# Front of a hybrid attention block: second-half transposes placed earlier, feature tiles copied and split in pairs; states of the linear heads split on DVE

## The chip, the cores and the metric

The kernel runs on one core of a Trainium2 chip. The engines are TensorE (PE, with its weight loads PEld), VectorE (DVE), ScalarE (ACT), GpSimd (POOL) and the queue that issues most loads (SP). Each engine works through its own instructions in order and waits on semaphores for the others. The metric is the device time of one execution in microseconds (us).

## What is computed

One block over 1024 tokens of width 1024, in fp32: a norm, one wide projection, three branches (retention, gated linear attention, windowed attention with sinks), gates, an output projection, and a feed-forward part.

```python
h = rmsnorm(x, norm_mix_pre)
proj = h @ w_in          # split into rq rk rv rg | gq gk gv gg ga | sq sk sv | gate_logits
o_ret = head_groupnorm(retention(rq, rk, rv)) * silu(rg)
o_gla = head_rmsnorm(gla(gq, gk, gv, log_a(ga))) * silu(gg)
o_swa = swa_sinks(sq, sk, sv, attn_sinks)
merged = sum(sigmoid(gate_logits) * einsum(branches, w_branch))
x = x + rmsnorm(merged @ w_out, norm_mix_post)
h = rmsnorm(x, norm_ffn_pre)
x = x + rmsnorm((silu(h @ ffn_w_gate) * (h @ ffn_w_up)) @ ffn_w_down, norm_ffn_post)
```

Retention and the gated branch go chunk by chunk: `state = decay * state + k^T v`, and each chunk's output adds `q` times the state before it.

## The kernel before, in words

Every fp32 operand of a matrix product is split into a high part (a cast on ACT, `fp32r`) and a low part (source minus high part, a subtraction on DVE); a product then takes three matmuls (high-high, high-low, low-high). The helper `split` does this at lines 127 and 128 of the profile.

**The front.** The 1024 tokens are two halves of 512 (`th` 0 and 1). For a half, four token tiles `x` are squared on ACT (`first_square`, which also sums), POOL makes `rstd`, DVE scales (`first_scale`, tile `xn`). PE then transposes to eight feature tiles (`k` 0 to 7): four 128x128 transposes fill one PSUM bank `xps`. `first_split` copies a bank to SBUF with the norm's gain (tile `hf`, odd `k` on DVE, even `k` on ACT) and splits it (tile `hT`: cast on ACT, subtraction on DVE). The products of the wide projection use a scheme with seven block products per pair of weight tiles ("key"); its steps are `p1` to `p7` with PSUM tiles `x`, `y`, `z`. They need splits of weight sums (`sums`: tiles `raw` and `s`) and of sums of the feature tiles of both halves (`t1` to `t4`; `make("t2")` makes `t2` first). `swa_values(t0)` makes the attention values of two token tiles: 48 matmuls of 272 columns into two banks `sv`, called four times (0, 2, 4, 6; the last two use the second half); ACT and DVE then split the result into `vhl`. In this front all engines keep the order in which the code is written (`e.on = True`), so its lines appear in the profile as L76. The order before is: first half, `p1` and `p2` of key 0 (the two `next(steps)`), split of the value weights on ACT and POOL, `swa_values(0)`, split of key 1's weights (`blocks`), `p1` and `p2` of key 1, `sums` of key 0, `swa_values(2)`, then the second half's eight transposed tiles with `sums` of key 1 in the middle, `t2`, `swa_values(4)`, `swa_values(6)`. After it, a scheduler orders the instructions.

**The linear heads.** Eight heads (four of retention, then four gated) run one after the other in `lin_head`, each over eight chunks. Per chunk DVE makes the new state `tmp` (tile `tu`, line 1041 or 1039) from the product `kv` and the state before; ACT makes its high part `us` (line 1045), DVE the low part (line 1046), POOL the scaled state `u` for the next chunk (line 1050). PE multiplies `us` with the queries of the next chunk (product `o<-us,q`). Between chunks `fill(1)` gives PE other products (values, or branch projections).

Of the kernel before, what the change touches and what calls it, by code (L numbers as in the profile page):

```python
# [11 lines left out]
AF = mybir.ActivationFunctionType  # L12
ALU = mybir.AluOpType
# [3 lines left out]
P = 128  # L17
# [3 lines left out]
NK = D // P  # L21
# [25 lines left out]
V_PRE, V_RW, V_RB, V_GW, V_FFN, V_BA, V_SNK, V_R, V_CAUSAL = 0, 8, 16, 24, 32, 40, 44, 60, 68  # L47
# [32 lines left out]
def block_kernel(ctx: ExitStack, tc: tile.TileContext, x, vecs, rows, alpha2, w_in, w_branch,  # L80
                 w_out, w_gate, w_up, w_down, cst_in, out):
    nc = tc.nc
    pe, ve, se, po = (Ordered(tc, e) for e in (nc.tensor, nc.vector, nc.scalar, nc.gpsimd))
# [15 lines left out]
    def bt(n, dt=F32):  # L99
        return bp.tile([P, TH], dt, name=f"{n}_{nid()}", tag="b")  # L100
# [7 lines left out]
    def bpair(n):  # L108
        t = dt_(n, F32R)
        return t[:, :TH], t[:, TH:]  # L110
# [3 lines left out]
    def bank(n):  # L114
        return psp.tile([P, TH], F32, name=f"{n}_{nid()}", tag="ps")
# [10 lines left out]
    def split(hi, lo, src, eng=None):  # L126
        se.copy(out=hi, in_=src)  # L127
        return (eng or ve).tensor_tensor(out=lo, in0=src, in1=hi, op=ALU.subtract)  # L128


    ident = const.tile([P, P], F32, name="ident")
    vec = const.tile([P, NVEC], F32, name="vec")
# [45 lines left out]
    def split_sv(raws):  # L178
        res = []
        for raw, kn in raws:  # L180
            wh, wl = wt_pair()
            split(wh[:, :kn * NSV], wl[:, :kn * NSV], raw[:, :kn * NSV], po)
            res += [(wh[:, k * NSV:(k + 1) * NSV], wl[:, k * NSV:(k + 1) * NSV]) for k in range(kn)]
        return res
# [102 lines left out]
    xT = [[None, None] for _ in range(NK)]  # L287
    hf = [[None, None] for _ in range(NK)]
# [9 lines left out]
    def first_square(xt):  # L298
        xn = dt_("xn")
        ms = sm("ms", 1)  # L300
        se.activation(out=xn, in_=xt, func=AF.Square, scale=1.0 / 32.0, accum_out=ms)
        return xn, rstd_of(ms, 1, EPS)
# [2 lines left out]
        ve.tensor_scalar(out=xn, in0=xt, scalar1=r, scalar2=None, op0=ALU.mult)  # L305
        return xn

    def first_split(k, th, ps):
        h = hf[k][th] = bt("hf")
        g = vec[:, V_PRE + k:V_PRE + k + 1]  # L310
        if k % 2:
            ve.tensor_scalar(out=h, in0=ps, scalar1=g, scalar2=None, op0=ALU.mult)
        else:
            se.activation(out=h, in_=ps, func=AF.Copy, scale=g)
        xT[k][th] = bpair("hT")
        split(*xT[k][th], h)


    ga = const.tile([P, NT, RANK], F32, name="ga")
# [2 lines left out]
    def swa_values(t0):  # L322
        ts = (t0, t0 + 1)
        pss = [bank("sv") for _ in ts]
        for k in range(NK):
            for t, ps in zip(ts, pss):
                hi, lo = (z[:, (t % 4) * P:(t % 4 + 1) * P] for z in xT[k][t // 4])
                mm3(ps[:, :NSV], (hi, lo), wsv[k], k == 0, k == NK - 1)
        v2 = dt_("vhl", F32R)
        for i, (t, ps) in enumerate(zip(ts, pss)):  # L330
            v = v2[:, i * TH:(i + 1) * TH].rearrange("p (g c) -> p g c", g=HKV)
            split(v[:, :, :DH], v[:, :, DH:], ps[:, :HKV * DH].rearrange("p (g c) -> p g c", g=HKV))
            ve.tensor_copy(out=ga[:, t, :], in_=ps[:, HKV * DH:NSV])
        po.dma_start(out=vhd[t0 // 2], in_=v2.bitcast(F32))
# [382 lines left out]
    inp = Pairs(mv, ikeys, in_load, in_out, 2, hsums)  # L717
# [11 lines left out]
    xns = []  # L729
# [5 lines left out]
        for k in range(NK):  # L735
            pe.transpose(out=pss[k][:, j * P:(j + 1) * P], in_=xns[j][:, k * P:(k + 1) * P], identity=ident)
    sq = []
    for k in range(NK):
        first_split(k, 0, pss[k])
        if k % 4 == 3:  # L740
            sq += [first_square(xt) for xt in xs2[k // 2 - 1:k // 2 + 1]]
    xns = [first_scale(xt, *q) for xt, q in zip(xs2, sq)]
    next(steps)
    next(steps)
    wsv = split_sv(wsv)
    swa_values(0)
    inp.blocks(ikeys[1])
    next(steps)
    next(steps)
    inp.sums(ikeys[0])  # L750
    swa_values(2)
    for k in range(NK):
        ps = bank("xps")
        for j in range(4):
            pe.transpose(out=ps[:, j * P:(j + 1) * P], in_=xns[j][:, k * P:(k + 1) * P], identity=ident)
        first_split(k, 1, ps)
        if k == 3:
            inp.sums(ikeys[1])
    inp.make("t2")
    swa_values(4)  # L760
    swa_values(6)
# [251 lines left out]
    def lin_head(br, h, st, fill):  # L1013
        if br == 0:
            to_end = lambda c: rret[:, h:h + 1]
            to_mid = lambda c: rret[:, H + h:H + h + 1]
        else:
            to_end = lambda c: gates_gla[h][0][:, c:c + 1]
            to_mid = lambda c: gates_gla[h][1][:, c + 1:c + 2]
        qs, ns, as_ = st["s"]  # L1020
        vs = st["v"]
        part = lambda pair, c: tuple(z[:, (c % 4) * P:(c % 4 + 1) * P] for z in pair[c // 4])
        u = uhl = None
        ys = [dt_("y"), dt_("y")]
        for c0 in range(0, NT, 2):
            pkv = bank("kv")
            po_ = bank("o")
            for c in (c0, c0 + 1):
                e = slice((c - c0) * DV, (c - c0 + 1) * DV)
                if c < NT - 1:  # L1030
                    mm3(pkv[:, e], part(ns, c), vs[c], True, True)
                mm3(po_[:, e], part(as_, c), vs[c], True, c == 0)
                if c:
                    mm3(po_[:, e], part(qs, c), uhl, False, True)
                if c < NT - 1:
                    tu = bt("tu")
                    tmp, un = tu[:, :DV], tu[:, DV:]
                    if u is None:
                        ve.tensor_scalar(out=tmp, in0=pkv[:, e], scalar1=to_end(c), scalar2=None, op0=ALU.mult)
                    else:  # L1040
                        ve.scalar_tensor_tensor(out=tmp, in0=pkv[:, e], scalar=to_end(c), in1=u,
                                                op0=ALU.mult, op1=ALU.add)
                    us = br_("us")
                    uhl = us[:, :DV], us[:, DV:]
                    se.activation(out=uhl[0], in_=tmp, func=AF.Copy, scale=to_mid(c))
                    ve.scalar_tensor_tensor(out=uhl[1], in0=tmp, scalar=to_mid(c), in1=uhl[0], op0=ALU.mult,
                                            op1=ALU.subtract)
                    if c < NT - 2:
                        u = un
                        po.tensor_scalar(out=u, in0=tmp, scalar1=to_mid(c), scalar2=to_end(c + 1),  # L1050
                                         op0=ALU.mult, op1=ALU.mult)
                if c == NT - 1:
                    se.copy(out=ys[1][:, 2 * DV:], in_=po_)
                fill(1)
            if c0 < NT - 2:
                se.copy(out=ys[c0 // 4][:, (c0 % 4) * DV:(c0 % 4 + 2) * DV], in_=po_)
            if c0 == 2:
                lin_norm(br, ys[0])
        lin_norm(br, ys[1])
        return [lambda th=th: lin_out(br, h, th, ys[th]) for th in range(2)]  # L1060
# [347 lines left out]
```

## Time and profile before

| | |
|---|---|
| median of 3 runs (lowest to highest) | 2171.03 us (2167.98 to 2172.43) |
| profiled execution: its time, its span | 2171.05 us, 2169.3 us |
| mean granted PE clock | 0.988 |
| PE busy | 2097.6 us (97%) |
| DVE, ACT, POOL busy | 1232.4 us (57%), 924.0 us (43%), 273.5 us (13%) |

The span runs from the first instruction to the last of the profiled execution. Busy time counts work alone, without waits. The granted clock is a share of TensorE's 2.4 GHz; 0.5 is its lower level, 1.2 GHz.

### The profile page before, as it was taken

The page shows a single profiled execution, that of the slowest core. Times are in us where ns is not written, and L with a number is a line of the kernel's source. Part 1 is how long each engine was busy: PE and PEld are TensorE (multiplying, and loading weights), DVE is VectorE, ACT ScalarE, POOL GpSimd, SP SyncE. Part 2 cuts the span into 40 slices and gives each one's busy share as a digit, 9 for nine tenths or more (in the row PEclk, how much of TensorE's full clock was granted, in tenths as well). Part 3 has the DMA queues.
Part 4 walks back from the last instruction along what each step waited for, and adds up shares of the span by engine and source line. Part 5 has one row for each costly group of instructions (what it writes and reads, how often), then busy time and mean ns, then how long its engine had stood idle before and what let it go on. Part 6 is the DMA issues. An engine that isn't in the chain of part 4 may idle for free. (4 is left out here: it accounts for less than half of the span.)

```text
span 2169.3 us, 28889 instructions
## 1 busy us (share of the span) xinstructions
PE 2097.6 (97%) x10612; PEld 1775.8 (82%) x10612; DVE 1232.4 (57%) x2263; ACT 924.0 (43%) x1800; POOL 273.5 (13%) x471
## 2 busy tenths in 40 slices
PE   6799999999999999999999999998999999999998
PEld 4678888888888899999788788876888888888886
DVE  4768764565443598755655744426765555553342
ACT  4446554334443577644533331145433333352240
POOL 2111000000000232232222210042000000000101
PEclk8999999999999999999999999999999999999999
DMA  4378665575556644576766654342454555574441
GB/s 150 116 225 262 195 193 161 183 228 180 171 156 191 215 149 149 176 244 238 271 226 234 221 178 134 107 126 88 134 154 132 139 146 141 149 278 142 154 171 39
DMA packets 351214, 376.64 MB, mean 174 GB/s; under 512 B 16848, under 2 KB 276304, under 8 KB 351072
## 3 DMA queue, kind: packets, MB, share of 16 engines
q1 hardware_dynamic: 309248, 273.59, 42.0%
q0 software_dynamic: 18208, 62.40, 7.6%
q10 hardware_dynamic: 23616, 38.81, 4.9%
q8 instruction: 83, 1.36, 0.3%
q14 instruction: 59, 0.48, 0.1%
HBM read 273.03 MB, written 101.71 MB: 173 GB/s over the span
## 5 line engine op out<-in xcount | busy, mean ns | idle before, releaser
L128 DVE TENSOR_TENSOR wl<-raw,wh 128x1024 fp32r<-128x1024 f32 x127 | 155.1, 1222 | 146.8 <-ACT wh L127 82.5
L127 ACT CAST s<-raw 128x512 fp32r<-128x512 f32 x216 | 130.1, 620 | 197.3 <-DVE raw L380 79.5
L127 ACT CAST wh<-raw 128x1024 fp32r<-128x1024 f32 x137 | 143.3, 1047 | 98.9 <-DMA raw<-in_w_down 52.0
L405 PE MATMUL x<-t,s 128*128 128x512 f32 x440 | 171.4, 392 | 5.6 <-ACT t L127 3.7
L406 PE MATMUL x<-t,s 128*128 128x512 f32 x440 | 172.8, 393 | 0.3 <-DVE t L128 0.3
L407 PE MATMUL x<-t,s 128*128 128x512 f32 x440 | 172.8, 393 | 0.4 <-DVE s L128 0.4
L355 ACT COPY sn<-x 128x512 f32<-128x512 f32 x163 | 95.2, 587 | 140.7 <-PE x L407 111.6
L241 PE MATMUL pf<-o,wh 128*128 128x512 f32 x384 | 149.8, 395 | 2.0 <-ACT o L127 2.0
L242 PE MATMUL pf<-o,wh 128*128 128x512 f32 x384 | 150.3, 392 | 0.4 <-DVE o L128 0.4
L128 DVE TENSOR_TENSOR s<-raw,s 128x512 fp32r<-128x512 f32 x216 | 145.4, 687 | 5.4 <-ACT s L127 4.6
L256 PE MATMUL v<-wh,hT 128*128 128x256 f32 x512 | 146.2, 285 | 0.0
L258 PE MATMUL v<-wh,hT 128*128 128x256 f32 x512 | 145.1, 283 | 0.0
L257 PE MATMUL v<-wl,hT 128*128 128x256 f32 x512 | 145.0, 283 | 0.0
L1340 PE MATMUL dn<-wl,f 128*128 128x512 f32 x352 | 136.3, 389 | 0.0
L1339 PE MATMUL dn<-wh,f 128*128 128x512 f32 x352 | 136.3, 389 | 0.0
L244 PE MATMUL pf<-o,wl 128*128 128x512 f32 x384 | 121.9, 391 | 0.0
L1342 PE MATMUL dn<-wh,f 128*128 128x512 f32 x352 | 108.7, 389 | 0.0
L405 PEld LDWEIGHTS x<-t,s 128*128 128x128 f32 x440 | 83.0, 189 | 24.0 <-ACT t L127 4.2
L257 PEld LDWEIGHTS v<-wl,hT 128*128 128x128 f32 x512 | 98.5, 192 | 1.1
L256 PEld LDWEIGHTS v<-wh,hT 128*128 128x128 f32 x512 | 98.4, 192 | 1.0
L258 PEld LDWEIGHTS v<-wh,hT 128*128 128x128 f32 x512 | 98.3, 192 | 0.1
L407 PEld LDWEIGHTS x<-t,s 128*128 128x128 f32 x440 | 83.5, 190 | 18.2 <-DVE s L128 0.8
(306 smaller groups left out, 5281.8 us busy)
## 6 DMA issues: line engine op xcount, KB each, us to landing
raw<-in_w_in SPq DMA_DIRECT2D x146, 512.0 KB, 6.0
raw<-in_w_down SPq DMA_DIRECT2D x44, 512.0 KB, 6.5
raw<-in_w_gate SPq DMA_DIRECT2D x43, 512.0 KB, 5.0
raw<-in_w_up SPq DMA_DIRECT2D x43, 512.0 KB, 4.6
v<-v POOLq DMA_DIRECT2D x32, 512.0 KB, 3.9
v<-v SPq DMA_DIRECT2D x32, 512.0 KB, 6.5
gT<-go ACTq DMA_DIRECT2D x48, 256.0 KB, 3.7
raw<-in_w_branch SPq DMA_DIRECT2D x24, 512.0 KB, 5.6
```

The source lines that it names most:

```text
L127: se.copy(out=hi, in_=src)
L128: return (eng or ve).tensor_tensor(out=lo, in0=src, in1=hi, op=ALU.subtract)
L241: pe.matmul(p_, lhsT=wh, rhs=hi, start=(k == 0), stop=False)
L242: pe.matmul(p_, lhsT=wh, rhs=lo, start=False, stop=False)
L256: pe.matmul(ps, lhsT=lh, rhs=rh, start=start, stop=False)
L257: pe.matmul(ps, lhsT=lh, rhs=rl, start=False, stop=False)
L258: pe.matmul(ps, lhsT=ll, rhs=rh, start=False, stop=stop)
L405: pe.matmul(ps, lhsT=h, rhs=hi, start=(start and k == 0), stop=False, skip_group_check=True)
L406: pe.matmul(ps, lhsT=h, rhs=lo, start=False, stop=False, skip_group_check=True)
L407: pe.matmul(ps, lhsT=l, rhs=hi, start=False, stop=(k == KH - 1), skip_group_check=True)
L1339: pe.matmul(ps[ch], lhsT=fh[:, ts_], rhs=ws[ch][0], start=(first and i == 0), stop=False)
L1340: pe.matmul(ps[ch], lhsT=fh[:, ts_], rhs=ws[ch][1], start=False, stop=False)
```

## The change

It does two things. In the front, `first_split` takes two banks: both are copied first (one on ACT, one on DVE), then both are split; a square of the second half follows every pair of the first half, in place of two squares behind every four tiles. The transposes of the second half are placed earlier: tiles 0 to 3 in front of `swa_values(0)`, tiles 4 to 7 in front of `p1` of key 1; `sums` of key 1 follows `swa_values(2)`. In `lin_head`, the high part of the state is made by DVE in place of ACT: 56 instructions of 128x256 (7 chunks of 8 heads).

```diff
-    def first_split(k, th, ps):
-        h = hf[k][th] = bt("hf")
-        g = vec[:, V_PRE + k:V_PRE + k + 1]
-        if k % 2:
-            ve.tensor_scalar(out=h, in0=ps, scalar1=g, scalar2=None, op0=ALU.mult)
-        else:
-            se.activation(out=h, in_=ps, func=AF.Copy, scale=g)
-        xT[k][th] = bpair("hT")
-        split(*xT[k][th], h)
+    def first_split(k0, th, pss):
+
+        for k, ps in zip((k0, k0 + 1), pss):
+            hf[k][th] = bt("hf")
+            g = vec[:, V_PRE + k:V_PRE + k + 1]
+            if k % 2:
+                ve.tensor_scalar(out=hf[k][th], in0=ps, scalar1=g, scalar2=None, op0=ALU.mult)
+            else:
+                se.activation(out=hf[k][th], in_=ps, func=AF.Copy, scale=g)
+        for k in (k0, k0 + 1):
+            xT[k][th] = bpair("hT")
+            split(*xT[k][th], hf[k][th])
...
-    for k in range(NK):
-        first_split(k, 0, pss[k])
-        if k % 4 == 3:
-            sq += [first_square(xt) for xt in xs2[k // 2 - 1:k // 2 + 1]]
+    for k in range(0, NK, 2):
+        first_split(k, 0, pss[k:k + 2])
+        sq.append(first_square(xs2[k // 2]))
...
+    def second_half(kk):
+        for k0 in kk:
+            pss = [bank("xps"), bank("xps")]
+            for k, ps in zip((k0, k0 + 1), pss):
+                for j in range(4):
+                    pe.transpose(out=ps[:, j * P:(j + 1) * P], in_=xns[j][:, k * P:(k + 1) * P], identity=ident)
+            first_split(k0, 1, pss)
+
     wsv = split_sv(wsv)
+    second_half((0, 2))
     swa_values(0)
     inp.blocks(ikeys[1])
+    second_half((4, 6))
     next(steps)
     next(steps)
     inp.sums(ikeys[0])
     swa_values(2)
-    for k in range(NK):
-        ps = bank("xps")
-        for j in range(4):
-            pe.transpose(out=ps[:, j * P:(j + 1) * P], in_=xns[j][:, k * P:(k + 1) * P], identity=ident)
-        first_split(k, 1, ps)
-        if k == 3:
-            inp.sums(ikeys[1])
+    inp.sums(ikeys[1])
     inp.make("t2")
...
-                    se.activation(out=uhl[0], in_=tmp, func=AF.Copy, scale=to_mid(c))
+                    ve.tensor_scalar(out=uhl[0], in0=tmp, scalar1=to_mid(c), scalar2=None, op0=ALU.mult)
```

Three places show how the rows on an engine move. First ACT in the first half, from its first copy out of PSUM; before:

```order
L76 ACTIVATE hf_291<-xps_251,vec 128x512
L76 CAST hT_293<-hf_291 128x512
L76 CAST hT_298<-hf_296 128x512
L76 ACTIVATE hf_301<-xps_253,vec 128x512
L76 CAST hT_303<-hf_301 128x512
L76 CAST hT_308<-hf_306 128x512
L76 ACTIVATE xn_311,ms_312<-x_198 128x1024
L76 ACTIVATE xn_317,ms_318<-x_200 128x1024
```

and in the changed kernel:

```order
L76 ACTIVATE hf_291<-xps_251,vec 128x512
L76 CAST hT_295<-hf_291 128x512
L76 CAST hT_298<-hf_293 128x512
L76 ACTIVATE xn_301,ms_302<-x_198 128x1024
L76 ACTIVATE hf_307<-xps_253,vec 128x512
L76 CAST hT_311<-hf_307 128x512
L76 CAST hT_314<-hf_309 128x512
L76 ACTIVATE xn_317,ms_318<-x_200 128x1024
```

ACT's own order within a pair stays; one square `xn` now follows each pair. On DVE (not shown) the odd tile's copy now stands ahead of the even tile's subtraction, where it stood behind it.

Second, ACT behind the second call of `swa_values`, whose result it casts to `vhl`; before, twelve rows of what follows:

```order
L76 CAST vhl_549<-sv_499 128x4x64
L76 CAST vhl_549<-sv_500 128x4x64
L76 ACTIVATE hf_562<-xps_557,vec 128x512
L76 CAST hT_564<-hf_562 128x512
L76 CAST hT_574<-hf_572 128x512
L76 ACTIVATE hf_582<-xps_577,vec 128x512
L76 CAST hT_584<-hf_582 128x512
L76 CAST hT_594<-hf_592 128x512
L76 CAST s_100_598<-raw_215 128x512
L76 CAST s_101_602<-raw_215 128x512
L76 ACTIVATE hf_612<-xps_607,vec 128x512
L76 CAST hT_614<-hf_612 128x512
```

and in the changed kernel:

```order
L76 CAST vhl_629<-sv_579 128x4x64
L76 CAST vhl_629<-sv_580 128x4x64
L76 CAST s_112_638<-raw_215 128x512
L76 CAST s_113_642<-raw_215 128x512
L76 CAST t_115_650<-t_114_647 128x512
L76 CAST t_117_656<-t_116_653 128x512
```

The copies `hf` and casts `hT` of the second half no longer stand between the values and `t2` (`t_115`); on DVE and PE it is the same.

Third, DVE in the last gated head, at the state of a chunk (`tu_12252`); before:

```order
L1041 SCALAR_TENSOR_TENSOR tu_12252<-kv_12241,end_2123,tu_12191 128x256
L128 TENSOR_TENSOR wl_12261<-raw_12258,wh_12260 128x1024
L1041 SCALAR_TENSOR_TENSOR tu_12287<-kv_12241,end_2123,tu_12252 128x256
L1046 SCALAR_TENSOR_TENSOR us_12254<-tu_12252,mid_2122,us_12254 128x256
L1046 SCALAR_TENSOR_TENSOR us_12289<-tu_12287,mid_2122,us_12289 128x256
```

and in the changed kernel:

```order
L1047 SCALAR_TENSOR_TENSOR tu_12252<-kv_12241,end_2123,tu_12191 128x256
L1051 TENSOR_SCALAR us_12254<-tu_12252,mid_2122 128x256
L128 TENSOR_TENSOR wl_12261<-raw_12258,wh_12260 128x1024
L1052 SCALAR_TENSOR_TENSOR us_12254<-tu_12252,mid_2122,us_12254 128x256
L1047 SCALAR_TENSOR_TENSOR tu_12287<-kv_12241,end_2123,tu_12252 128x256
L1051 TENSOR_SCALAR us_12289<-tu_12287,mid_2122 128x256
L1052 SCALAR_TENSOR_TENSOR us_12289<-tu_12287,mid_2122,us_12289 128x256
```

The high part (L1051) stands right behind the state, and the low part ahead of the next state. Before, the high part stood on ACT, where four scalings of `y` (line 992) were ahead of it at this place.

## Rows read from the trace of the kernel before

**Rows 1.** Page, part 1: busy time of each engine.

```profile
PE 2097.6 (97%) x10612; PEld 1775.8 (82%) x10612; DVE 1232.4 (57%) x2263; ACT 924.0 (43%) x1800; POOL 273.5 (13%) x471
```

**Rows 2.** Busy us of PE, PEld, DVE, ACT, POOL by stretch; clock, DMA share, GB/s.

```profile
35.00:43.30 8.30, 8.28 (x47) 8.06 (x47) 0.44 (x1) 0.36 (x1) 3.53 (x2) 0.71 0.01 2
43.30:58.80 15.50, 13.59 (x73) 11.78 (x74) 6.03 (x11) 3.33 (x7) 0.75 (x1) 0.89 0.08 34
58.80:78.00 19.20, 10.06 (x58) 8.63 (x57) 12.97 (x23) 9.11 (x16) 4.88 (x9) 0.73 0.37 138
78.00:95.70 17.70, 15.82 (x102) 13.84 (x100) 17.42 (x34) 8.19 (x17) 1.63 (x3) 1.00 0.37 116
95.70:140.00 44.30, 44.30 (x198) 36.13 (x199) 30.78 (x49) 21.57 (x38) 6.07 (x12) 1.00 0.74 227
905.00:1260.00 355.00, 345.13 (x2259) 308.89 (x2259) 212.81 (x443) 154.44 (x285) 97.88 (x173) 1.00 0.69 237
```

**Rows 3.** PE's longest wait from 40 us on, in the waits up to 96 us.

```profile
PE sv L76 <- ACT hf L76: 4.7, 1, 4.7
```

**Rows 4.** Timeline, first half: first copy, last low part, last square.

```profile
13.75 0.69 ACT L76 ACTIVATE hf<-xps,vec 128x512 f32<-128x512 f32 x1 [0.36 <-PE xps L76]
...
29.06 0.69 DVE L76 TENSOR_TENSOR hT<-hf,hT 128x512 fp32r<-128x512 f32 x1 [0.68 <-ACT hT L76]
...
29.98 1.04 ACT L76 ACTIVATE xn<-x 128x1024 f32<-128x1024 f32 x1
```

**Rows 5.** Groups by form, 0 to 96 us: high parts, scalings (count | busy, mean ns | idle before).

```profile
L76 ACT CAST hT<-hf 128x512 fp32r<-128x512 f32 x16 | 9.9, 618 | 12.2 <-DVE hf L76 11.9
...
L76 DVE TENSOR_SCALAR xn<-x,rstd 128x1024 f32<-128x1024 f32 x8 | 7.6, 956 | 11.5 <-POOL rstd L76 11.5
```

**Rows 6.** Timeline at 33 to 35 us: POOL's split, the last scaling, PE's start.

```profile
32.97 5.56 POOL L76 TENSOR_TENSOR wl<-raw,wh 128x816 fp32r<-128x816 f32 x3
33.05 2.39 DVE L76 TENSOR_SCALAR xn<-x,rstd 128x1024 f32<-128x1024 f32 x1 [0.77 <-POOL rstd L76]
34.95 0.59 PE L76 MATMUL sv<-wl,hT 128*128 128x272 f32 x1 [2.14 <-POOL wl L76]
```

**Rows 7.** Timeline of PE: third projection group, second transposes, the late z product.

```profile
52.69 0.28 PE L76 MATMUL sv<-wh,hT 128*128 128x272 f32 x1
...
58.70 2.47 PE L76 MATMUL xps<-ident,xn 128*128 128x128 f32 x20
...
95.69 0.50 PE L407 MATMUL z<-t,s 128*128 128x512 f32 x1 [1.00 <-DVE s L128]
```

**Rows 8.** Timeline of DVE: sums of key 1 begin, t2 begins, t2's last part.

```profile
66.65 0.68 DVE L76 TENSOR_TENSOR raw<-raw,raw 128x512 f32<-128x512 f32 x1
...
71.93 0.69 DVE L76 TENSOR_TENSOR hT<-hf,hT 128x512 fp32r<-128x512 f32 x1
...
77.85 0.69 DVE L76 TENSOR_TENSOR t<-hf,hf 128x512 f32<-128x512 f32 x1
...
90.29 0.68 DVE L76 TENSOR_TENSOR t<-t,t 128x512 fp32r<-128x512 f32 x1
```

**Rows 9.** PE's longest wait from 905 to 1260 us.

```profile
PE o L256 <- ACT us L1045: 4.8, 5, 1.8
```

**Rows 10.** Durations (min/median/max ns): ACT's split, POOL's u, a DVE scaling.

```profile
L1045 ACT ACTIVATE us<-tu,vec x28: 493/510/523, 916.4 to 1067.1; 128x256 fp32r<-128x256 f32 x28
...
L1050 POOL TENSOR_SCALAR tu<-tu,vec x24: 547/560/2297, 916.5 to 1056.7; 128x256 f32<-128x256 f32 x24
...
L866 DVE TENSOR_SCALAR lg<-lg,rs x128: 275/347/551, 726.3 to 901.2; 128x256 f32<-128x256 f32 x112, 128x128 f32<-128x128 f32 x16
```

**Rows 11.** Timeline, last head: the state, ACT's scalings of y, the late split.

```profile
1244.51 0.45 DVE L1041 SCALAR_TENSOR_TENSOR tu<-kv,end,tu 128x256 f32<-128x256 f32 x1
...
1247.64 1.70 ACT L992 ACTIVATE y<-y,rstd 128x256 f32<-128x256 f32 x4 [5.43 <-POOL rstd L141]
...
1249.25 0.89 ACT L1045 ACTIVATE us<-tu,mid 128x256 fp32r<-128x256 f32 x2
```

## The prediction

> **What bounds the kernel now.** I read the page first: PE is busy for 2097.6 us, 97% of the span [rows 1], so a change can only pay in the few places where PE waits or runs at its lower clock. The busy time by stretch shows one such place at the front [rows 2]: from 58.8 to 78 us PE is busy for 10.06 of 19.2 us at a mean granted clock of 0.73, a mixture of its two levels, 1.2 and 2.4 GHz. The list of PE's waits names what it waits for there: the values of the third token pair (`sv`) for the copies `hf` of the second half, 4.7 us in one piece [rows 3]. In the next stretch, up to 95.7 us, PE still waits now and then, and DVE is busy for 17.42 of 17.7 us: it makes `t2` and the splits behind it, so DVE's place in its queue sets when PE can go on. From 95.7 to 140 us PE has no gap at all (44.30 of 44.30 us) at full clock [rows 2]. So whatever brings the product at 95.69 us [rows 7] forward is carried on to the end. The second place is the stretch of the linear heads, where PE is busy for 345.13 of 355 us [rows 2] and its longest wait is for `us` from ACT, 4.8 us in five pieces [rows 9].
>
> **Part 1, the front.** I follow the chain in the new order, with durations of the old rows.
>
> First half. Before, copies and splits of the eight tiles run from 13.75 to 29.75 us and the last square ends at 31.02 [rows 4]. ACT's casts spend 11.9 us waiting for copies that DVE makes one subtraction late [rows 5]. With both copies ahead of the splits ACT has no such gap, and it is the longer queue: per pair a copy (0.69), two casts (0.62 each) and a square (1.04), 2.97 us. Four pairs from 13.75 end at 25.6: 5.4 us earlier.
>
> Last scaling. It started at 33.05, while POOL had begun to split the value weights at 32.97, and took 2.39 us [rows 6]; the other seven take (7.6 - 2.39)/7 = 0.74 us each [rows 5]. Shifted by 5.4 it starts at 27.65, again beside POOL. I take 2.39 again, the nearest row, so it ends at 30.0; the other bound, 0.74, would give 1.65 us more.
>
> Tiles 0 to 3 of the second half. Two pairs without squares: 2 x (0.69 + 0.62 + 0.62) = 3.9 us on ACT, done at about 34.9 with the last low part. PE needs only the transposes, some 2.6 us of them behind the last scaling, and starts the values (0) at 32.6 where it had started at 34.95 [rows 6]. Those 48 matmuls took up to 43.3 us at clock 0.71 [rows 2]; the group from 52.69 to 58.70 took 6.0 at full clock [rows 7]. With PE at work since 30.0 I take 7, so they end at 39.6 (bounds 6 and 8.3).
>
> Key 1 and values (2). Before, PE waited for the split of key 1's weights behind 43.3, did 24 products and was through at 52.69: 9.4 us. Now 16 transposes lie in that wait (20 take 2.47 us [rows 7], so 2.0); the products at full clock cost 24 x 44.3/198 = 5.4 [rows 2], and I leave 0.7 of the wait. The values follow with 6.0: 39.6 + 2.0 + 0.7 + 5.4 + 6.0 = 53.7, where it was 58.7. Tiles 4 to 7 are copied and split beside these products, on ACT and DVE, which were busy for only 3.33 and 6.03 us in 43.3 to 58.8 [rows 2]; without that cover they would put 2 x 1.93 = 3.9 us ahead of `t2`.
>
> `t2`. Behind the values (2) DVE had the second half's tiles with the sums of key 1 in their middle, and began `t2` only at 77.85 [rows 8]. Now only the sums are left (5.3 us, 66.65 to 71.93) and the values' own split (estimate 1.2, four short operations). `t2` itself takes 13.1, from 77.85 to 90.97 [rows 8]. So it ends at 53.7 + 1.2 + 5.3 + 13.1 = 73.3, which is 17.7 us earlier. What stands behind it is in the same order, so the product that waits for `s` at 95.69 comes at 78.0.
>
> What is given back. PE now finishes the values (6) at 53.7 + 12 = 65.7 and waits between the parts of `t2`, so I expect one spell at 1.2 GHz more behind it. The stretch at clock 0.89, with waits of PE at its start, lost at most 15.5 x 0.11 = 1.7 us by the lower level; the one at 0.73 lost at most 19.2 x 0.27 = 5.2, half of it in gaps [rows 2]. I take 2.2. Part 1: -17.7 + 2.2 = -15.5 us. Its best end has the short scaling, the values (0) at 6 and no spell: -20.3. Its worst is that only PE's gaps from 58.8 to 78 go: 19.2 - 10.06 = -9.1. The writes of `hT` by POOL also start earlier, ahead of the values' writes; their data are there by 34.9, so they hold nothing.
>
> **Part 2, the heads.** Removed: 56 operations of 0.51 us on ACT; added: 56 on DVE. This trace has no such operation in the heads; the nearest row is a DVE scaling of the same shape, 0.35 us at the median [rows 10], so DVE gets 19.6 us more in 355, where it is busy for 212.81 [rows 2]. Behind the new instruction on DVE wait the low part, the next state and splits for other products. The gain: ACT takes its instructions in order, and at the end of the last head the state is there at 1244.96, but four scalings of `y`, which wait for POOL's `rstd`, come first at 1247.64, and `us` starts only at 1249.25 [rows 11]. On DVE it would start at 1245. At most the 4.8 us of this wait go; at the other end all 19.6 us lie on PE's path. Since PE has other products between chunks, I take -3.5, and for the range -4.8 to +3.
>
> POOL's `u` starts from the same state as the moved operation, and takes 0.56 us [rows 10]. The last scaling of the front shows what an overlap with POOL costs DVE: 2.39 in place of 0.74 us. The Trainium skill (Advanced Engine Details and Errata, "VectorE Performance Modes", Mode Summary) says that DVE's second port is shared with GpSimd, that DVE's two-port modes and GpSimd's instructions block each other, and that such a mode wants source and result in SBUF, as they are here. By that rule this part is no gain but the loss that stands below as a rival; the trace agrees with it in that one row. The scalings of the same shape at 0.275 to 0.551 us [rows 10] show no such hold in their length, so I leave it at a small chance.
>
> **Sum.** The profiled execution took 2171.05 us (span 2169.3 and 1.75 around it), next to the median of 2171.03. 2171.05 - 15.5 - 3.5 = 2152 us.
>
> **The rivals.**
> (a) As forecast: 2152, with a range of its own from 2146 to 2158. Chance 0.70.
> (b) The front gives less: the spells at the lower clock come at the key's products too, or DVE reaches `t2` later, so that little more than PE's gaps goes, and the heads give nothing: 2171 - 9.1 = 2162. For it: the clock fell behind a short wait at the same weights before (0.89). Against it: 16 transposes now stand there. Chance 0.17.
> (c) The change doesn't do what it says, because the gain is given back before 140 us: DVE, busy for 30.78 of 44.3 us there, or the loads of the next weights set the pace. For it: DMA is at 0.74 in that stretch. Against: PE has no gap there, and loads start when buffers come free, which also comes earlier. Between 2168 and 2171. Chance 0.08.
> (d) Slower, by one mechanism: the moved operation is held by POOL's `u` for its 0.56 us and then needs 0.35, so 0.91 us of DVE's queue per chunk. If PE pays all of it, 56 x 0.91 = 51 us; half of it, 25, gives 2171 - 15.5 + 25 = 2181. It decides from 0.35 us per chunk on, since 56 x 0.35 = 19.8 is what outweighs part 1 and 0.2%. Against: PE's own work between chunks. Chance 0.05.
>
> **How the numbers follow.** 0.2% of 2171 is 4.3 us, about what a measurement of this kernel can tell from no change. Cases (a) and (b) are faster, 0.87; (c) is the same, 0.08; (d) is slower, 0.05. The range takes in the best ends of both parts (2171 - 20.3 - 4.8 = 2146) and (b) with a loss of 3 in the heads (2171 - 9.1 + 3 = 2165); (c) and (d) lie outside.
>
> **What would show it.** In the changed profile the last square of the second half should end near 25.6 us, the values (0) near 39.6, `t2` near 73, and the product that waits for `s` should start near 78 to 80 (95.69 before). The stretch from 58.8 to 78 should hold no wait for `hf`. In the heads no wait of PE for ACT's `us` is left, and the moved operation takes about 0.35 us; a median near 0.9 would speak for (d). The forecast fails if PE meets new gaps between 80 and 125 us, if the lower clock covers more than about 5 us behind `t2`, or if PE's waits for `us` from DVE add up to more than 4.8 us.

## The result and the profile after

The changed kernel takes 2147.78 us (median of 4 runs, 2146.75 to 2148.81), the kernel before 2169.66 us beside it: a ratio of 0.9898, 95% interval 0.9887 to 0.991. That is 21.9 us less, where 19 were forecast; the time lies within the likeliest case's own range. The profiled execution took 2147.92 us with a span of 2146.1, so the two profiled spans differ by 23.2 us.

The page of the changed kernel, part 1 (busy time of each engine), answers to [rows 1]:

```profile
PE 2086.7 (97%) x10612; PEld 1769.6 (82%) x10612; DVE 1254.4 (58%) x2319; ACT 898.4 (42%) x1744; POOL 277.4 (13%) x471
```

PE does the same 10612 matmuls in 10.9 us less busy time, so about half of the 23.2 us is shorter matmuls (the mean granted clock is 0.995, 0.988 before), the rest gaps that went. DVE has the 56 instructions that ACT lost. Busy time by stretch, with the columns and the first five bounds of [rows 2]:

```profile
35.00:43.30 8.30, 7.84 (x49) 6.71 (x48) 6.25 (x13) 5.84 (x10) 2.14 (x5) 1.00 0.67 249
43.30:58.80 15.50, 15.50 (x122) 15.30 (x121) 10.59 (x20) 3.85 (x7) 0.53 (x1) 1.00 0.09 35
58.80:78.00 19.20, 15.10 (x68) 10.88 (x67) 18.99 (x37) 8.95 (x19) 1.82 (x4) 0.92 0.39 123
78.00:95.70 17.70, 17.70 (x78) 14.30 (x77) 12.94 (x21) 9.65 (x18) 2.05 (x4) 0.99 0.52 163
95.70:140.00 44.30, 41.89 (x179) 33.43 (x178) 27.73 (x45) 17.53 (x31) 5.99 (x12) 0.96 0.77 239
883.40:1238.40 355.00, 346.15 (x2276) 310.96 (x2275) 237.21 (x503) 130.35 (x233) 102.57 (x173) 1.00 0.70 239
```

The third stretch had 10.06 us of PE at 0.73 before; now it has 15.10 at 0.92, and DVE is busy all the time in it. The two stretches ahead of it, at 0.71 and 0.89 before, run at full clock. PE's waits up to 96 us, its longest four and the one for the late product:

```profile
PE xps L76 <- DVE xn L76: 10.5, 4, 7.9
PE x L76 <- ACT hT L76: 1.3, 2, 0.7
PE y L76 <- ACT hT L76: 1.3, 2, 0.6
PE z L408 <- ACT s L127: 1.2, 1, 1.2
...
PE z L410 <- DVE s L128: 1.0, 1, 1.0
```

The wait for `hf` [rows 3] is gone; every wait above 1.2 us now lies in the first 29 us. The timeline of the front, one row for each step that the prediction times:

```profile
23.68 1.05 ACT L76 ACTIVATE xn<-x 128x1024 f32<-128x1024 f32 x1
24.50 4.39 DVE L76 TENSOR_SCALAR xn<-x,rstd 128x1024 f32<-128x1024 f32 x4
26.30 5.70 POOL L76 TENSOR_TENSOR wl<-raw,wh 128x816 fp32r<-128x816 f32 x3
28.94 1.64 PE L76 MATMUL xps<-ident,xn 128*128 128x128 f32 x13 [1.99 <-DVE xn L76]
30.34 0.37 PE L76 MATMUL sv<-wh,hT 128*128 128x272 f32 x1
36.30 0.29 PE L76 MATMUL sv<-wh,hT 128*128 128x272 f32 x1
56.73 0.68 DVE L76 TENSOR_TENSOR t<-hf,hf 128x512 f32<-128x512 f32 x1
69.16 0.68 DVE L76 TENSOR_TENSOR t<-t,t 128x512 fp32r<-128x512 f32 x1
74.56 0.63 PE L410 MATMUL z<-t,s 128*128 128x512 f32 x1 [1.00 <-DVE s L128]
```

The last square ends at 24.7 us (31.02 before), the values (0) run from 30.34 to 36.6, `t2` from 56.73 to 69.84 (77.85 to 90.97 before [rows 8]), and the product that waits for `s` comes at 74.56, 21.1 us earlier than at 95.69 [rows 7].

Where the span's 23.2 us come from is read from the first and last start of two matmul groups, the heads' `kv` and the output projection's transposes `h2t` (columns: duration min/median/max in ns, first and last start in us). Before:

```profile
L256 PE MATMUL kv<-v,n x56: 277/283/415, 915.4 to 1251.6; 128*128 128x256 f32 x56
...
L1250 PE MATMUL h2t<-ident,xn x64: 270/272/328, 1434.8 to 1502.2; 128*128 128x128 f32 x64
```

After:

```profile
L256 PE MATMUL kv<-v,n x56: 277/283/418, 896.0 to 1230.0; 128*128 128x256 f32 x56
...
L1256 PE MATMUL h2t<-ident,xn x64: 270/273/330, 1413.2 to 1479.0; 128*128 128x128 f32 x64
```

The heads begin 19.4 us earlier and end 21.6 earlier; `h2t` begins 21.6 earlier and ends 23.2 earlier, which is the difference of the spans. So: 19.4 from the front, 2.2 in the heads, and 1.6 in a stretch that the change doesn't touch.

That 1.6 is clock. Behind `h2t` PE waits for `x` from DVE, 1.81 us before and 1.80 after, in the same order. Busy time by stretch around this wait, before:

```profile
1437.00:1440.00 3.00, 1.48 (x5) 1.02 (x6) 1.41 (x2) 0.00 (x0) 2.04 (x3) 0.88 1.14 311
1440.00:1443.00 3.00, 3.00 (x9) 2.40 (x8) 0.00 (x0) 1.94 (x6) 2.28 (x4) 0.55 1.19 300
```

And after, shifted by 21.6 us:

```profile
1415.40:1418.40 3.00, 1.49 (x6) 1.08 (x7) 1.41 (x2) 0.00 (x0) 2.05 (x3) 1.00 1.17 315
1418.40:1421.40 3.00, 3.00 (x15) 2.46 (x14) 0.00 (x0) 1.93 (x6) 2.28 (x4) 1.00 1.21 302
```

The granted clock falls to 1.2 GHz behind the wait in one trace (3.00 x 0.12 + 3.00 x 0.45 = 1.7 us lost) and not in the other.

The heads: PE's waits there (885 to 1240 us), the first three, for [rows 9]:

```profile
PE o L257 <- DVE us L1052: 2.8, 5, 1.3
PE pf L242 <- DVE o L128: 2.5, 2, 2.0
PE pf L241 <- ACT o L127: 1.2, 1, 1.2
```

The wait of 4.8 us for ACT's `us` is gone; 2.8 for DVE's low part stand in its place (0.2 before). The waits for `o` grew as well, from 2.4 us in three pieces to these 3.7. The moved operation and POOL's `u` in the first four heads, for [rows 10]:

```profile
L1051 DVE TENSOR_SCALAR us<-tu,vec x28: 345/353/577, 897.6 to 1046.9; 128x256 fp32r<-128x256 f32 x28
...
L1056 POOL TENSOR_SCALAR tu<-tu,vec x24: 548/718/2300, 897.2 to 1036.5; 128x256 f32<-128x256 f32 x24
```

And the timeline at the place of [rows 11]:

```profile
1223.21 0.48 DVE L1047 SCALAR_TENSOR_TENSOR tu<-kv,end,tu 128x256 f32<-128x256 f32 x1
1223.72 0.35 DVE L1051 TENSOR_SCALAR us<-tu,mid 128x256 fp32r<-128x256 f32 x1
1223.79 0.72 POOL L1056 TENSOR_SCALAR tu<-tu,mid,end 128x256 f32<-128x256 f32 x1 [1.00 <-DVE tu L1047]
...
1225.51 1.23 DVE L128 TENSOR_TENSOR wl<-raw,wh 128x1024 fp32r<-128x1024 f32 x1 [1.43 <-ACT wh L127]
1226.65 0.48 DVE L1052 SCALAR_TENSOR_TENSOR us<-tu,mid,us 128x256 fp32r<-128x256 f32 x1
...
1227.18 0.39 PE L257 MATMUL o<-us,q 128*128 128x256 f32 x1 [1.31 <-DVE us L1052]
```

The high part starts right behind the state, no longer behind ACT's scalings of `y`; but the low part stands behind a weight split `wl` of 1.23 us in DVE's queue, and PE waits 1.31 us for it. The wait moved from the high part to the low part. Of the 2.58 us between them (1224.07 to 1226.65) DVE stood idle for 1.43, because that split waits for ACT's cast `wh`: what ACT does late still reaches PE, now through DVE's queue.

In the next chunk nothing stands between the two parts, and the low part runs beside POOL's `u`:

```profile
1227.56 0.35 DVE L1051 TENSOR_SCALAR us<-tu,mid 128x256 fp32r<-128x256 f32 x1
1227.62 0.72 POOL L1056 TENSOR_SCALAR tu<-tu,mid,end 128x256 f32<-128x256 f32 x1 [3.11 <-DVE tu L1047]
...
1227.95 0.66 DVE L1052 SCALAR_TENSOR_TENSOR us<-tu,mid,us 128x256 fp32r<-128x256 f32 x1
```

It takes 0.66 us here and 0.48 at 1226.65, with no `u` beside it. On the mean the 56 low parts went from 516 and 501 ns (first and last four heads) to 578 and 556, some 3.3 us more in all. With the 20.6 us of the moved operations, DVE is busy for 224.02 us from the first `kv` to the last, where it was 201.64.

### The profile page after: what moved, and what is told of

Its sections match the earlier page's. It is cut to its first block, busy times and chain, and to the rows that moved or that the text cites. A ratio compares the mean times of both kernels' runs of the same rounds, so it can differ in the third digit from the quotient of the medians.

```text
span 2146.1 us, 28876 instructions
## 1 busy us (share of the span) xinstructions
PE 2086.7 (97%) x10612; PEld 1769.6 (82%) x10612; DVE 1254.4 (58%) x2319; ACT 898.4 (42%) x1744; POOL 277.4 (13%) x471
## 5 line engine op out<-in xcount | busy, mean ns | idle before, releaser
L408 PEld LDWEIGHTS x<-t,s 128*128 128x128 f32 x440 | 82.8, 189 | 25.8 <-ACT t L127 4.2
L409 PEld LDWEIGHTS x<-t,s 128*128 128x128 f32 x440 | 83.6, 190 | 19.9 <-DVE t L76 1.9
L256 PEld LDWEIGHTS v<-wh,hT 128*128 128x128 f32 x512 | 98.3, 192 | 1.0
L410 PEld LDWEIGHTS x<-t,s 128*128 128x128 f32 x440 | 83.6, 190 | 18.3 <-DVE s L128 0.8
```

The lines of the kernel that those rows point to most:

```text
L256: pe.matmul(ps, lhsT=lh, rhs=rh, start=start, stop=False)
L408: pe.matmul(ps, lhsT=h, rhs=hi, start=(start and k == 0), stop=False, skip_group_check=True)
L409: pe.matmul(ps, lhsT=h, rhs=lo, start=False, stop=False, skip_group_check=True)
L410: pe.matmul(ps, lhsT=l, rhs=hi, start=False, stop=(k == KH - 1), skip_group_check=True)
```

## The experiments

The theory: the front's gain is DVE's chain behind the values (0), brought forward by the time PE starts them, plus full clock in these products; the heads' gain is ACT's wait alone. Rivals: one half of the front's edit does all; DVE's new time in the heads is paid by PE; the front's length is set by something else. Each kernel ran beside the kernel before on its chip; ratios are to that.

**The two parts apart.** e1 is the kernel before with the heads' line, e2 the changed kernel without it:

```diff
# e1: the kernel before, and
-                    se.activation(out=uhl[0], in_=tmp, func=AF.Copy, scale=to_mid(c))
+                    ve.tensor_scalar(out=uhl[0], in0=tmp, scalar1=to_mid(c), scalar2=None, op0=ALU.mult)
# e2: the changed kernel, and this line the other way round
```

e1: 

> The kernel before with the heads' part alone (the high part of the state on DVE). My theory: PE's 4.8 us of waits for ACT's us go, a part of it comes back as waits for DVE, and the time falls by 2 to 3.5 us, to 2166 to 2168 beside 2169.7. Rival (the moved operation is held by POOL's u, 0.91 us per chunk): the operation's median is near 0.9 us and the time rises by 5 us or more. Rival (no effect): within 1 us, and the rest of the change's 21.9 us lies in the front.

e2: 

> The changed kernel with ACT making the high part again, so the front's part alone. My theory: the product that waits for s stands at 74.6 us as in the changed kernel, and the time falls by 18 to 20 us, to about 2150 to 2152. Rival (the heads gave more than their waits show, the front less): above 2154. Together with the heads alone the two should add up to the 21.9 us of the whole change within 2 us, if they don't touch each other.

e1 takes 2166.17 us, ratio 0.9981 (0.9972 to 0.999); e2 2153.18, ratio 0.9922 (0.9909 to 0.9934). That is 3.9 and 16.9 us, together 20.8 of the 21.9; 2 to 3.5 and 18 to 20 had been expected. The `kv` of e1 run from 913.1 to 1247.0 us, so the heads' own stretch, 336.2 us before, is shorter by 2.3, about what the changed kernel shows (2.2). Its profiled execution, 2164.92 us, gains 2.3 us more ahead of the heads, where its code is that of before, and 1.6 by lacking the clock spell behind `h2t` (65.7 us from its first to its last, as in the changed kernel), where its code is that of before too. e2 keeps PE's old wait:

```profile
PE o L256 <- ACT us L1051: 4.8, 5, 1.8
```

So this wait belongs to the heads' line and to nothing in the front. e2 falls short by the clock: in its trace it is 0.66 from 30 to 35 us, where the changed kernel has 1.00, and the late product comes at 76.13, not at 74.6 as expected.

**The front's two edits apart**, both with the heads as before. e3 has the moved transposes, with tiles copied and split singly and two squares behind every four tiles. e4 has the pairs, with transposes and sums in their old places:

```diff
# e3: the changed kernel, with first_split and the squares as before, and in second_half
-            first_split(k0, 1, pss)
+            first_split(k0, 1, pss[0])
+            first_split(k0 + 1, 1, pss[1])
# e4: the changed kernel, and
-    second_half((0, 2))
...
-    second_half((4, 6))
...
-    inp.sums(ikeys[1])
+    for k0 in range(0, NK, 2):
...
+        first_split(k0, 1, pss)
+        if k0 == 2:
+            inp.sums(ikeys[1])
```

e3: 

> The front's new places alone: tiles copied and split one by one, two squares behind every four tiles, as before; transposes and sums of key 1 at their new places; ACT makes the heads' high part. My theory: the first half and the last scaling end as before (35.4 us), a pair takes 3.27 in place of 2.0 us, t2 begins near 65.5 (77.85 before, 56.7 in the changed kernel), and the time falls by about 10 us. Rival (the places bring all of it, the pairs only fill time that nobody waits for): 18 us or more. Rival (the places bring nothing without the pairs): under 3 us.

e4: 

> The pairs alone: tiles of both halves copied and split in twos, a square behind every pair of the first half, but the second half's transposes and the sums of key 1 at their old places; ACT makes the heads' high part. My theory: the last square ends near 25.4 in place of 31.0 us, the four pairs of the second half save 4 x 1.3 us, t2 begins near 68, and the time falls by about 9 to 10 us. Rival (the places bring all of it): under 3 us. Rival (the pairs bring all of it): 18 us or more.

e3 takes 2156.55 us, ratio 0.9941 (0.9927 to 0.9955); e4 2159.28, ratio 0.9951 (0.9938 to 0.9963): 13.6 and 10.8 us. The late product in the timeline of e3:

```profile
82.50 0.50 PE L407 MATMUL z<-t,s 128*128 128x512 f32 x1 [0.99 <-DVE s L128]
```

and of e4:

```profile
83.47 0.50 PE L410 MATMUL z<-t,s 128*128 128x512 f32 x1 [0.99 <-DVE s L128]
```

Alone, they bring it forward by 13.2 and 12.2 us; together, in e2, it stands at 76.13, 19.6 earlier, so some 6 us of the two are the same time (the clock differs too: 0.77, 0.82 and 0.89 from 30 to 45 us in e3, e4 and e2). e3 gained 3.6 us more than I had expected of it, e4 about 1 more. Neither does all.

**DVE's time in the heads.** e6 issues the moved operation twice per chunk:

```diff
                     ve.tensor_scalar(out=uhl[0], in0=tmp, scalar1=to_mid(c), scalar2=None, op0=ALU.mult)
+                    ve.tensor_scalar(out=uhl[0], in0=tmp, scalar1=to_mid(c), scalar2=None, op0=ALU.mult)
```

> The changed kernel with the moved operation issued twice per chunk (the second writes the same values again): 56 more of 0.35 us, 19.8 us more on DVE in the heads. Theory (PE has cover between chunks, and DVE's time there is mostly not on PE's path): 0 to 4 us slower than the changed kernel, so 2148 to 2152, and PE's waits for us from DVE grow from 2.8 to at most 6 us. Rival (DVE's time in the heads is paid by PE, and the move gained only because ACT's wait was worse): 15 to 20 us slower, 2163 to 2168. If POOL's u is what pays for DVE's operations, its median rises again, from 0.72 towards 0.9 us; otherwise it stays at 0.72.

2155.68 us, ratio 0.9931 (0.9919 to 0.9944): 7.9 us above the changed kernel (7.2 by the ratios), between the two theories. The heads in its trace:

```profile
L256 PE MATMUL kv<-v,n x56: 274/283/415, 896.2 to 1235.6; 128*128 128x256 f32 x56
```

339.4 us in place of 334.0, so 5.4 us, 0.1 per chunk, came onto PE's path where 19.8 were added, and up to 1.7 of that is a longer spell at 1.2 GHz (the clock is 0.66 from 1025 to 1035 us, 0.83 in the changed kernel); another 1.5 is the clock spell behind `h2t`, which this trace has (67.3 us, as before the change). PE's waits for `us` are 2.1 and 1.4, hardly more. The cover that I counted on is there, but it isn't whole: a fifth to a quarter of what DVE is given in the heads is paid. POOL's `u` stays at 718 ns, so a second DVE operation costs POOL nothing more. DVE pays: the second operation, now the one that runs beside `u`, takes 0.43 us on the mean, the first 0.36, and the low part behind them is back at 0.49.

**What makes the second half's scalings long.** e9 asks for POOL's split of the value weights to be issued behind the last scaling; e10 makes POOL read the last scaled tile first. e5 is the changed kernel again.

```diff
# e9
-            split(wh[:, :kn * NSV], wl[:, :kn * NSV], raw[:, :kn * NSV], po)
+            se.copy(out=wh[:, :kn * NSV], in_=raw[:, :kn * NSV])
+            with tc.issue_after(scaled[-1].ins):
+                po.tensor_tensor(out=wl[:, :kn * NSV], in0=raw[:, :kn * NSV], in1=wh[:, :kn * NSV], op=ALU.subtract)
...
# e10
+    held = sm("held", 1)
+    po.tensor_scalar(out=held, in0=xns[-1][:, :1], scalar1=1.0, scalar2=None, op0=ALU.mult)
     wsv = split_sv(wsv)
```

e5: 

> The changed kernel once more, on the chip of the next run, as its reference. Both theories: within 2 us of 2147.8. If low-clock spells behind short waits come by chance, its profile may have one where the first profile of it had none, or the other way round, at unchanged order: about 1.6 us for a spell of 3.3 us at half clock.

e9: 

> The changed kernel with POOL's three subtractions for the value weights held until the last of the four scalings of the second half has been issued. Theory (POOL's running subtraction is what makes DVE's scaling take longer): the four scalings take 4 x 0.74 = 3.0 us in place of 4.39, PE's wait of 1.99 us for the last one falls to about 0.6, and values (0) start about 1.4 us earlier, but the second low part then comes behind the start, so that up to 1.4 us goes back as a wait for wl; the time within 1.5 us of the changed kernel. Rival (the last scalings are long by themselves, for the memory of the fourth token tile or their wait for rstd): the four still take about 4.4 us, and only PE's wait for wl is new, so 1 to 1.5 us slower.

e10: 

> The changed kernel with one small POOL operation (128x1) that reads the last of the four scaled tiles, ahead of POOL's subtractions for the value weights: these now can't begin before the scalings are done. Theory (a subtraction running on POOL is what lengthens DVE's scaling): the four scalings take 3.0 us in place of 4.39, PE's wait of 1.99 us for the last one falls to about 0.6, values (0) start 1.4 us earlier, and up to 1.4 us of that goes back as a new wait for wl; time within 2 us of 2148. Rival (the last scalings are long by themselves): the four still take about 4.4 us, and the wait for wl comes on top, 1 to 1.5 us slower.

e12, which is e10 again: 

> The kernel with POOL held behind the scalings once more, since the same kernel with the held t4 came out 3.1 us apart in two submissions. Theory (the 1.5 us of shorter scalings stay, and what else it gained, some 2 us, is low-clock spells that come by chance): the four scalings again 2.9 us, the z product near 73.6 or, with a spell before it, up to 2.5 us later; time between 2144 and 2147.5. Rival (the whole gain belongs to the order): 2144 to 2145 again.

e5 takes 2148.46 us, ratio 0.9899 (0.9882 to 0.9917), as the changed kernel did. Its clock is that of the first profile too (0.66 from 74 to 79 us, 0.94 from 110 to 140), so these two traces don't show a spell that comes and goes in one kernel; e7 and e11, below, do. e9 says nothing on POOL: the edit fixed an order of issue, and POOL, which had nothing to wait for, began its split at 26.41 us all the same; the scalings took 4.39. It takes 2148.35, ratio 0.9895 (0.9879 to 0.9911). In e10 POOL waits, and the timeline shows it:

```profile
24.17 2.90 DVE L76 TENSOR_SCALAR xn<-x,rstd 128x1024 f32<-128x1024 f32 x4
...
27.12 1.64 PE L76 MATMUL xps<-ident,xn 128*128 128x128 f32 x13 [0.49 <-DVE xn L76]
27.15 0.25 POOL L76 TENSOR_SCALAR held<-xn 128x1 f32<-128x1 f32 x1 [0.88 <-DVE xn L76]
27.37 6.06 POOL L76 TENSOR_TENSOR wl<-raw,wh 128x816 fp32r<-128x816 f32 x3
28.51 0.37 PE L76 MATMUL sv<-wh,hT 128*128 128x272 f32 x1
29.34 0.39 PE L76 MATMUL sv<-wl,hT 128*128 128x272 f32 x1 [0.45 <-POOL wl L76]
```

The four scalings take 2.90 us in place of 4.39, PE's wait for the last falls from 1.99 to 0.49, and the price is a wait of 0.45 for `wl`. That is close to the theory (3.0, about 0.6, and up to 1.4 given back), and the rival, scalings that are long by themselves, is out. The time is 2144.19 us, ratio 0.9881 (0.9864 to 0.9897), and again as e12 2142.24, ratio 0.9865 (0.9848 to 0.9881), both below what the theory had said (within 2 us of 2148, and 2144 to 2147.5). Its eight runs lie at 2141.65 to 2144.74, the eight of the changed kernel at 2146.75 to 2149.32. So this version beats the changed kernel, by 3.6 to 6.2 us in the medians, more than the 1.5 of the scalings; the late product comes at 73.56, only 1.0 us earlier. Its trace shows where some of the rest lies: in 110 to 140 us PE is busy for 28.84 us at full clock, where the changed kernel has 27.59 at 0.94, because there it waits 1.59 us for `s` at 124.62 and here 0.34:

```profile
122.41 0.50 PE L408 MATMUL x<-t,s 128*128 128x512 f32 x1 [0.34 <-ACT s L127]
```

That the shorter wait is what keeps the clock up isn't shown: e9 has a wait of 1.81 us there and e7, below, one of 1.40, and both ran at 1.00 from 110 to 140 us. The profiled execution of e9, with the scalings as long as ever, took 2144.82 us. So of e10's gain what comes before the late product is explained, and the rest may be clock.

**The chain behind `t2`.** The scheduler had put the four subtractions that make `t4` (line 584) into DVE's chain from `t2` to the split `s` of the late product. e7 holds them behind the last split of `t1` in the front, e8 in the feed-forward's up projection too, and e11 is e7 again:

```diff
...
-                ve.tensor_tensor(out=o, in0=o, in1=t2, op=ALU.subtract)
+                if self.late:
+                    with tc.issue_after(self.last.ins):
+                        ve.tensor_tensor(out=o, in0=o, in1=t2, op=ALU.subtract)
...
-    hsums = Sums(hf)
+    hsums = Sums(hf, True)
```

e7: 

> The changed kernel, with the four subtractions that make t4 held behind the last split of t1 in the front; the scheduler had put them in the middle of DVE's chain from t2 to the split s that the late z product waits for. Theory (DVE's chain behind the values (2) sets when PE goes on, and what it gains is kept): four operations of about 0.6 us leave the chain, the z product comes 2.4 us earlier, near 72.2 us, and the time falls by 2 to 2.5 us, to about 2145.5. Rival (PE is held by its own queue or the loads by now, so the end of DVE's chain is no longer what counts): the z product moves, but the time stays within 0.5 us of the changed kernel, 2147.8.

e8: 

> As the experiment before it, and the same held subtractions in the feed-forward's up projection. Theory (that projection's DVE chain sets PE's pace there as in the front): a further 0 to 2.4 us off, 2143 to 2146. Rival (the sums of the feed-forward are ready long before PE needs them, or a late t4 now holds the steps that use it): the same as the front alone, or slower by up to 2 us.

e11: 

> The kernel of the held t4 once more, to see which part of its gain of 2.3 us is the earlier product and which is a low-clock spell that was missing in its first profile. Theory (the z product is 1.0 us earlier, and the spell between 110 and 140 us of the changed kernel, 1.8 us, goes with the new order): z product near 73.5, no low clock in 110 to 140 us, time 2145 to 2146. Rival (the spell comes by chance): the z product again near 73.5, but the spell back in some executions, and times of 2145 to 2148.

e7 takes 2145.45 us, ratio 0.9885 (0.987 to 0.99); e8 2146.48, ratio 0.9888 (0.9875 to 0.9902), so the second stage adds nothing, as the rival had it; e11 2148.57, ratio 0.9899 (0.9884 to 0.9914). e7 had met its forecast to the tenth, and for the wrong reason: the product came only 1.0 us earlier (73.53; 72.2 expected), and e11, the same kernel, is 3.1 us longer, above what its theory (2145 to 2146) and its rival (up to 2148) had said, with the product at 75.04. Their difference is in the clock, 1.2 GHz at other places. In e11 PE's transposes behind the last scaling ran slow:

```profile
28.83 3.04 PE L76 MATMUL xps<-ident,xn 128*128 128x128 f32 x13 [1.99 <-DVE xn L76]
```

3.04 us in place of 1.64, behind the same wait of 1.99 us, and the granted clock was 0.54 from 30 to 35 us, 0.83 in e7 and 1.00 in the changed kernel. So holding `t4` isn't shown to gain anything.

## Why the prediction was right, step by step

**Part 1, the front: right in its mechanism, one term too large.** The chain went the way that the working followed: the copies of a pair ahead of its splits shortened the first half, the moved tiles took the wait for `hf` away, and `t2` followed the sums alone. Against the changed kernel's rows:

- Last square: 25.6 forecast, 24.7 measured. Last scaling: 30.0 forecast, 28.9 measured. That its length beside POOL's split is a cost of the overlap was read from one row, and e10 shows it.
- The values (0) are the term that was mis-sized. They were to start at 32.6 and take 7 us; they started at 30.34 and ended at 36.6. Of the 3.0 us at their end, 1.1 is the earlier scaling, 1.2 the transposes behind it (2.6 charged, from no row; 1.4 measured from 28.94 to 30.34), and 0.7 the products (7 charged, 6.25 measured). The last two are clock, and in part luck: the stretch ran at 1.00. e11 shows the case that I had priced: there the clock is 0.54 from 30 to 35 us, the transposes take 2.7 us, and the same products start at 31.52 and take 7.6, to 39.1. e2 and e7 have part of such a spell there too (0.66 and 0.83).
- From there on the sums held: from the end of the values (0) to the start of `t2` 20.6 us were forecast (14.1 for key 1 and the values (2), 1.2 and 5.3 for the split and the sums) and 20.1 measured, 36.6 to 56.73; `t2` took 13.1 as before. It ended at 69.84 (73.3 forecast), and the product stood at 74.56 (78.0).
- Given back: 2.2 forecast, 1.7 measured (21.1 at the product, 19.4 at the heads). The spell at 1.2 GHz that I expected behind `t2` is there, from about 75 to 78 us. In e9 the front runs in the same order and the same time, and its spell is missing; so the term was a guess at whether a spell comes, and in the changed kernel it did. The clock of both, from 74 to 79 us, first the changed kernel:

```profile
74.00:79.00 5.00, 4.44 (x12) 3.49 (x13) 4.62 (x8) 2.66 (x6) 1.16 (x2) 0.66 0.43 164
```

and e9:

```profile
74.00:79.00 5.00, 4.33 (x19) 3.57 (x20) 4.62 (x9) 2.65 (x5) 1.06 (x2) 1.00 0.44 166
```

**One sign of failure came up and was none.** PE has a new gap of 1.59 us at 124.62, inside the stretch that I had named. It is no new wait: the kernel before has its wait for ACT's `s` (1.3 us) and a clock of 0.83 between 140 and 150 us, and both came 19 us earlier with all the rest.

**Part 2, the heads: right in its sign, 1.3 us too large.** 3.5 forecast, 2.2 measured by the heads' own stretch, 2.3 in e1. The term that was mis-sized is the price of DVE's time, for which 1.3 of the 4.8 us were left. The high part starts at once, as I said, and takes 0.35 us, but the low part behind it now stands in a queue that is 22.4 us fuller (19.6 forecast): 2.8 us of waits for it came in place of the 0.2 before, and the waits for `o` grew by 1.3. e6 puts the price there at a fifth to a quarter of what is added. From the first `kv` to the last, PE's idle time fell by 1.0 us (9.87 to 8.85) and its busy time by 1.2 (326.33 to 325.15); why its products got shorter isn't settled.

**Outside both parts:** 1.6 us less, which no step had. It is the clock behind `h2t`. With it the errors add up to the 4.2 us by which the span fell further than forecast: -3.4 at the product, -0.5 given back, +1.3 in the heads, -1.6 here.

**Two readings that were off and moved no term.** The 11.9 us of ACT's waits for DVE's copies [rows 5] cover both halves. In the first half alone they are 5.7 us, and 0.1 in the changed kernel, which bears the shorter first half out. And 56 x 0.35 is 19.6, not 19.8.

**The rivals.** (b), a front worth only PE's gaps, fell with e2 (16.9 us) and with the clock of 1.00 where it had expected spells. (c), all given back before 140 us, fell with the `kv` rows. (d), DVE held by POOL's `u`, fell in its size: the moved operation's median is 353 ns, not 0.91 us. But a hold there is: the low part behind it pays some 3.3 us in all, and POOL's `u` from the same state went from 560 to 718 ns, off PE's path (DVE's waits for it fell from 7.1 to 2.6 us). So by the rule that I had weighed (the Trainium skill, Advanced Engine Details and Errata, "VectorE Performance Modes", Mode Summary: the two block each other) the trace agrees that there is interference; in the front DVE's last scaling pays for it, in the heads POOL's `u` and DVE's low part.

## What to carry to other kernels

Follow a chain from engine to engine through its queues, and price a step by the rows of the same instructions at either clock level, and say which the sum takes: a spell at the lower level that one execution has stays away in the next. When an operation moves to another engine, look at what then stands behind it there: here the wait moved from the high part to the low part, and less than half of it went. Before a gain of one or two microseconds is put down to an edit, look whether the granted clock differs in a stretch that the edit doesn't touch.

## What the runs showed of the hardware that I had not expected

- The same wait of PE, in the same order, is followed by 1.2 GHz in one trace and by 2.4 in another. Behind `h2t` (wait 1.79 to 1.81 us) a spell of about 3 us stands in the kernel before, e3, e4 and e6, and none in the other ten traces. At 74 us it stands in the changed kernel and e5 and not in e9. Each is worth about 1.6 us, and e7 and e11, one kernel, are 3.1 us apart. What decides isn't shown.
- Where DVE and POOL work at once, the operation that started second is the long one in these rows. In the front POOL's split starts at 26.30 us and DVE's last scaling at 26.64: the scaling takes 2.24 of the 4.39 us of the four, and in e10, where POOL starts behind it, the four take 2.90. In the heads the moved operation starts first and keeps its 353 ns; POOL's `u`, 0.06 us behind it, takes 0.72 us in place of 0.56, and DVE's low part, which starts while `u` runs, 0.66 in place of 0.48. e10 changes the order in the front alone; in the heads no run does.
- A second DVE operation of 19.8 us in all, given to an engine busy for two thirds of the stretch, cost 5.4 us of PE's time although PE's listed waits hardly grew. PE's idle time between the first `kv` and the last grew by 2.0 us and its busy time by 3.4, of which the longer spell at 1.2 GHz accounts for up to 1.7; the rest isn't settled.
